# Side splits on GpSimd's queue, the second memory's K/V product at the first norm boundary, and index queries first in the mixing

## The chip, the cores and the metric

The kernel is one program on one core of a Trainium2 chip. The metric is device microseconds (us) of one execution. Matrix products run on TensorE (PE); VectorE (DVE), ScalarE (ACT) and GpSimd (POOL) do the rest, and SyncE (SP) issues most of the DMAs. Each engine takes its instructions in program order and waits at the head of its own queue; an instruction that cannot start holds up all behind it on that engine.

## The reference, cut to what matters

Two transformer blocks run one after the other on 512 tokens of width 1024, all in float32:

```python
h = rmsnorm(x, g_pre_mix)                    # block one
proj = h @ w_in                              # conv, q, k, v, memory q, three gates
merged = sigmoid(ga)*y_a + sigmoid(gb)*y_b + sigmoid(gc)*y_c
x = x + rmsnorm(merged @ w_out, g_post_mix)  # first norm boundary
h = rmsnorm(x, g_pre_ffn)
u = causal_dwconv(h @ w_up, ffn_conv_w, ffn_conv_b)
x = x + rmsnorm((gelu(a) * g) @ w_down, g_post_ffn)
h = rmsnorm(x, norm_mix)                     # block two
hq, hf, hi, hg, sq, sk, sv, iq, ik, iw, mq = split(h @ w_in_2)
o_hg = hgrn2_mix(hq, hf, hi, hg)             # gated recurrence
o_sa = dsa_mix(sq, sk, sv, iq, ik, iw)       # index scores choose the keys
o_mem = mem_mix(mq, rmsnorm(mem_2), w_mem_kv_2)
x = x + concat(o_hg, o_sa, o_mem) @ w_out_2
x = x + (silu(a) * b) @ w_ffn_out_2
```

## The kernel before, in words

Every float32 product is made of three TensorE passes over parts (L175 to L177): each operand is split into a rounded "hi" and the rest "lo". `load` (L189) brings a 512 KB weight tile into `r`, one of three raw buffers, on SP's queue. `split` then makes `wh` on ACT (L203) and `wl` on DVE (L204); there are three pairs of them. A raw buffer is free again when its `wl` is made, and a pair is free when TensorE is done with the tile three before.

The class `Program` holds the work as a list of jobs, which set the order in which instructions are written out. Before each job it splits weights up to two tiles ahead (four for the resident tiles of a `head_chunks`, six for those at the end of a `gemm_out`) and loads up to three more. A job writes its matrix product in pieces; after each piece comes a tick (`tick`), at which every background generator started by `pr.start(name, gen, rate)` takes `rate` steps. One tick is 6 matrix passes of 512 columns. `pr.drain(name)` steps the generators, with nothing between the steps, until that one has ended.

The weights of block two's mixing are split ahead of time, as side work: `Parts.make` (L212) loads a tile (L216), waits four steps, splits it on ACT (L218) and DVE (L219), waits three steps, writes both parts to a DRAM buffer `wd` (L221, L222) and the generator `splits` adds two steps. So a tile takes 9 ticks. When the mixing uses such a tile, `split` loads its parts from `wd` (L199, L200).

The stages around the change, with their place in the profiled execution: the third gate pass (378 to 441 us: eight times a gate chunk of 24 passes and a `w_mem_out` chunk of 12, with six side splits in the background, then `pr.drain("splits")`), `w_out` (441 to 494), the first norm boundary, the up projection (44 chunks of 24 passes, to 796, with 23 more side splits), the down projection, the second norm boundary, and the mixing (936 to 1195). A norm boundary: the last four jobs of `gemm_out` each end one 128-token tile, whose `epi1` normalises it (ACT L260, POOL L251, DVE L341). `next_head` then runs the first four chunks in two halves of 256 columns, and the transposes of the last two token tiles (L330) come inside it. The second memory's rows are normalised and transposed by `memT2.build`, started at up chunk 2; their K/V product `w_mkv2` (48 passes) runs at up chunk 6, after `pr.drain("memT2")`. In the up projection POOL makes the hi part of each result (L183), on which DVE's L180 waits.

Of the kernel before, what the change touches and what calls it, by code (L numbers as in the profile page):

```python
# [143 lines left out]
def body(tc, ctx, io):  # L144
# [62 lines left out]
    class Parts:  # L207
# [5 lines left out]
        def make(self):  # L213
            raw, hi, lo = slot([P, 1024]), slot([P, 1024], F32R), slot([P, 1024], F32R)
            self.d = drp.tile([2, P, 1024], F32, name=nm("wd"))
            nc.sync.dma_start(raw, self.src)  # L216
            yield from wait(4)
            a_.copy(hi, raw)  # L218
            v_.tensor_tensor(out=lo, in0=raw, in1=hi.bitcast(F32), op=ALU.subtract)  # L219
            yield from wait(3)  # L220
            nc.sync.dma_start(self.d[0], hi.bitcast(F32))  # L221
            nc.sync.dma_start(self.d[1], lo.bitcast(F32))  # L222

    pr = Program(load, split)

# [608 lines left out]
    def gate(br, m, use):  # L834
        def f(ps):
            th = tmp()
            a_.activation(th, ps, AF.Tanh, scale=0.5, bias=hbg[:, br * 8 + m:br * 8 + m + 1])
            st["th"] = th
        chunk(io["w_in_gate"][br * 8 + m], H, f)
        x = (cvx, oT, omT)[br]  # L840
        chunk(io[("w_conv_out", "w_attn_out", "w_mem_out")[br]][m], lambda: x, use, nk=4)
# [8 lines left out]
    def use_bc(m, last):  # L850
        def f(ps):
            z, dst = tmp(), mg[m // 2][:, m % 2, :]
            v_.scalar_tensor_tensor(z, st.pop("th"), 1.0, ps, op0=ALU.add, op1=ALU.mult)
            g_.tensor_tensor(out=dst, in0=dst, in1=z, op=ALU.add)
            if last:
                merged.put(m, dst)
        return f
# [23 lines left out]
    M = {n: [Parts(io[n][j]) for j in range(io[n].shape[0])]  # L881
         for n in ("w_hf", "w_hq", "w_iq", "w_mqsv", "w_sqk", "w_hi", "w_hg")}
    M["w_ikw"] = [Parts(io["w_ikw"])]
    order = [M[n][c] for n in ("w_hf", "w_hq") for c in (0, 1)] + M["w_ikw"] + M["w_iq"] + M["w_mqsv"]
    order += [M[n][c] for n in ("w_hf", "w_hq") for c in (2, 3)] + M["w_sqk"] + M["w_hi"] + M["w_hg"]

    def splits(a, b):
        def g():
            for p in order[a:b]:
                yield from p.make()  # L890
                yield from wait(2)
        return g
# [1 line left out]
    for m in range(KD):  # L894
        gate(1, m, use_bc(m, False))
    pr.drain("mem")
    pr.start("splits", splits(0, 6))
    for m in range(KD):
        gate(2, m, use_bc(m, True))
    pr.drain("splits")  # L900


    def post_norm(gpost, gpre, half):

        d = {}

        def setup():
            d["sq"] = cst.tile([P, NT], F32, name=nm("sqA"))
            d["hn"] = Act(KD)

        def epi0(t, ps):
            if t == 0:
                setup()
                d["post"], d["pre"] = load_gain(gpost), load_gain(gpre)
            if t % 2 == 0:
                d["f", t // 2] = slot([P, 2, 512])
            a_.activation(tmp(), ps, AF.Square, scale=half / 32, accum_out=d["sq"][:, t:t + 1])
            v_.tensor_tensor(out=d["f", t // 2][:, t % 2, :], in0=ps, in1=d["post"][:, 0:512], op=ALU.mult)

        def epi1(t, ps):  # L920
            sqB = small(1)
            a_.activation(tmp(), ps, AF.Square, scale=half / 32, accum_out=sqB)
            rs = rsqrt_small(1, [d["sq"][:, t:t + 1], sqB], 1.0, post=None if half == 1.0 else half)
            f1 = tmp()
            v_.tensor_tensor(out=f1, in0=ps, in1=d["post"][:, 512:D], op=ALU.mult)
            sq = []
            for hf, f in ((0, d["f", t // 2][:, t % 2, :]), (1, f1)):
                x = xs[t][:, hf * 512:hf * 512 + 512]
                v_.scalar_tensor_tensor(x, f, rs, x, op0=ALU.mult, op1=ALU.add)
                sq.append(ssq(x, 1 / 32))  # L930
            ys[t] = norm_y(xs[t], sq, d["pre"])

        def late(t):
            norm_T(ys.pop(t), put_h(d["hn"], t))

        def swap():
            st["h"] = d["hn"]
        return epi0, epi1, late, swap

    def next_head(late, srcs, uses, after=None):  # L940

        hooks = {(0, 0): late[1], (0, 2): lambda: late[0](2), (0, 3): lambda: late[0](3)}
        if after is not None:
            hooks[1, 1] = after
        head_chunks(srcs, H, uses, hooks)

    e0, e1, late, swap = post_norm("g_post_mix", "g_pre_ffn", 0.5)
    gemm_out(lambda hf, j: io["w_out"][hf * 4 + j], 4, lambda: merged, e0, e1, late=late)

# [11 lines left out]
    def use_up_a(j):  # L961
        def f(ps):
            ff[j] = ffn_conv(j, ps)
            a_.activation(ff[j], ff[j], AF.Gelu_apprx_tanh)
        return f
# [6 lines left out]
        return f  # L972

    W = io["w_up"]
    next_head((late, swap), [W[0], W[NFF], W[1], W[NFF + 1]], [use_up_a(0), use_up_g(0), use_up_a(1), use_up_g(1)])
    pr.start("splits", splits(6, len(order)))
    for j in range(2, NFF):
        if j == 2:
            pr.start("memT2", lambda: memT2.build())
        if j == 6:  # L980
            pr.drain("memT2")
            gemm_N([io["w_mkv2"][i] for i in range(4)], lambda: memT2, lambda t, ps: use_mkv2(t, ps), nt=2)
            pr.start("kv2", lambda: fin_mkv2())
        chunk(W[j], H, use_up_a(j))
        chunk(W[NFF + j], H, use_up_g(j))

# [512 lines left out]


    def mixing():
        next_head((late2, swap2), [M[n][c] for n in ("w_hf", "w_hq") for c in (0, 1)],
                  [use_hf(0), use_hf(1), use_hq(0), use_hq(1)], park)
        pr.start("gates0", gates(0))
        pr.start("hgrn", hgrn_levels, 0.6)
        chunk(M["w_ikw"][0], H, use_ikw)
        pr.start("idx", chain(sel0, index_weights, *(index_scores(c) for c in range(4)), top_keys(3),
                              top_keys(2), top_keys(1)), 1.0)
        for c in range(4):
            chunk(M["w_iq"][c], H, use_iq(c))  # L1510
        gemm_N(M["w_mqsv"], H, use_mqsv)
        pr.ctl(load_kv2)
        pr.start("finm", fin_mq)
        for c in (2, 3):
            chunk(M["w_hf"][c], H, use_hf(c))
        pr.drain("finm")
        pr.start("mem2", chain(mem2_pair(0), mem2_pair(1)), 0.5)
        for c in (2, 3):
            chunk(M["w_hq"][c], H, use_hq(c))
        pr.start("gates1", gates(1))  # L1520
        gemm_N(M["w_sqk"], H, use_sqk)
        pr.start("fin", fin_sqk)
        gemm_N(M["w_hi"], H, use_hi)
        pr.start("tail0", hgrn_tail(0))
        pr.start("sa", chain(sa_pair(0), sa_pair(1)), 0.5)
        pr.start("tail1", hgrn_tail(1))
        for c in range(4):
            chunk(M["w_hg"][c], H, use_hg(c))
# [180 lines left out]
```

## Time and profile before

| what | value |
|---|---|
| median of 3 runs | 1606.48 us (1604.28 to 1608.55) |
| the profiled execution | 1602.35 us |
| its span, first to last instruction | 1600.6 us |
| TensorE busy | 1533.0 us, 96% of the span |
| VectorE / ScalarE / GpSimd busy | 786.4 / 595.9 / 185.3 us |
| mean granted TensorE clock | 0.98 |
| DMA | 215.82 MB, mean 135 GB/s |

TensorE is busy nearly all the time, so a saving has to come from its idle time, from its time at the lower clock (a granted clock of 0.5 is 1.2 GHz, 1.0 is 2.4 GHz), or from fewer passes. What matters of the other engines is whom they keep waiting.

### The profile page before, as it was taken

The numbers are of one execution on the slowest core, as the hardware profiler recorded it, in microseconds if no ns is written. First come the engines' busy times: TensorE is split into PE (matmuls) and PEld (weight loads), VectorE is DVE, ScalarE is ACT, GpSimd is POOL, SyncE is SP. The second block draws the span as 40 slices with busy tenths as digits, with TensorE's granted clock in tenths as the row PEclk, the third lists the DMA queues.
The fourth block names the chain that finished last, engine by engine and source line by source line (L and its number), as shares of the span: only waits on it lengthen the run. The fifth ranks groups of instructions, "written<-read, shape, count | busy, mean of one in ns | idle before, by whom it ended". The sixth has DMA issues, their size and how long they took to land.

```text
span 1600.6 us, 20603 instructions
## 1 busy us (share of the span) xinstructions
PE 1533.0 (96%) x8107; PEld 1265.8 (79%) x8107; DVE 786.4 (49%) x1216; ACT 595.9 (37%) x1039; POOL 185.3 (12%) x325
## 2 busy tenths in 40 slices
PE   8999999999998889988999999998989999999999
PEld 7887888888778768767878897776868988888887
DVE  5455454554355666565633337996455333333231
ACT  5454453443344434333423245444543222222120
POOL 1000000131112100000000115434200000000000
PEclk9999999999999989999999999998999999999999
DMA  5322233323652356654565523432323222222331
GB/s 186 105 93 86 79 126 119 105 82 136 217 208 69 132 192 230 209 197 177 205 233 200 224 86 128 176 141 98 112 94 117 71 101 93 99 98 93 105 119 53
DMA packets 63623, 215.82 MB, mean 135 GB/s; under 512 B 7428, under 2 KB 7940, under 8 KB 63526
## 3 DMA queue, kind: packets, MB, share of 16 engines
q1 hardware_dynamic: 59040, 206.60, 36.4%
q10 hardware_dynamic: 4486, 7.90, 1.8%
q8 instruction: 64, 1.05, 0.3%
q14 instruction: 33, 0.27, 0.1%
HBM read 177.64 MB, written 36.83 MB: 134 GB/s over the span
## 4 chain that ended last, share of the span: by engine, by line
PE 39%; DVE 6%; DMA 4%; ACT 4%; issue 2%; POOL 2%; SPq 0%; ACTq 0%; POOLq 0%; DVEq 0%
PE p L175 12%; PE p L176 12%; PE p L177 12%; DMA s<-w_sqk 2%; DMA s<-w_hi 1%; DVE wl L204 1%; PE p L330 1%; DVE s L1053 1%; DMA s<-w_hq 1%; DVE m L1052 1%; ACT s L218 1%; ACT s L615 0%; POOL m L251 0%; DVE s L219 0%; POOL s L183 0%
## 5 line engine op out<-in xcount | busy, mean ns | idle before, releaser
L175 PE MATMUL p<-s,wh 128*128 128x512 f32 (+1 forms) x1224 | 481.0, 393 | 5.6 <-ACT wh L203 5.5
L177 PE MATMUL p<-s,wl 128*128 128x512 f32 (+1 forms) x1224 | 476.6, 389 | 8.8 <-DVE wl L204 8.8
L176 PE MATMUL p<-s,wh 128*128 128x512 f32 (+1 forms) x1224 | 475.9, 389 | 0.0
L204 DVE TENSOR_TENSOR wl<-r,wh 128x1024 fp32r<-128x1024 f32 x208 | 245.3, 1184 | 273.4 <-ACT wh L203 272.6
L177 PEld LDWEIGHTS p<-s,wl 128*128 128x128 f32 x1224 | 231.6, 189 | 59.2 <-DVE wl L204 11.7
L203 ACT CAST wh<-r 128x1024 fp32r<-128x1024 f32 x208 | 206.1, 996 | 191.6 <-PE p L176 180.2
L175 PEld LDWEIGHTS p<-s,wh 128*128 128x128 f32 x1224 | 231.8, 189 | 53.2 <-ACT wh L203 7.3
L176 PEld LDWEIGHTS p<-s,wh 128*128 128x128 f32 x1224 | 231.7, 189 | 44.7
L175 PE MATMUL p<-wh,s 128*128 128x512 f32 x512 | 207.3, 405 | 6.5 <-ACT wh L203 5.3
L176 PE MATMUL p<-wl,s 128*128 128x512 f32 x512 | 204.6, 400 | 7.7 <-DVE wl L204 7.7
L177 PE MATMUL p<-wh,s 128*128 128x512 f32 x512 | 203.8, 398 | 0.0
L176 PE MATMUL p<-s,s 128*128 128x256 f32 (+1 forms) x408 | 132.0, 324 | 4.6 <-DVE s L180 4.6
L175 PE MATMUL p<-s,s 128*128 128x256 f32 (+1 forms) x408 | 133.0, 326 | 2.2 <-ACT s L291 2.1
L177 PE MATMUL p<-s,s 128*128 128x256 f32 (+1 forms) x408 | 131.4, 322 | 0.0
L175 PEld LDWEIGHTS p<-wh,s 128*128 128x128 f32 x512 | 98.9, 193 | 29.6 <-ACT wh L203 6.2
L176 PEld LDWEIGHTS p<-wl,s 128*128 128x128 f32 x512 | 99.0, 193 | 29.2 <-DVE wl L204 9.3
L177 PEld LDWEIGHTS p<-wh,s 128*128 128x128 f32 x512 | 98.8, 193 | 21.2
L183 POOL TENSOR_SCALAR s<-t 128x512 fp32r<-128x512 f32 (+1 forms) x64 | 34.6, 541 | 663.2 <-DVE t L1574 227.4
L176 PEld LDWEIGHTS p<-s,s 128*128 128x128 f32 x408 | 79.4, 194 | 10.9 <-DVE s L180 5.6
L175 PEld LDWEIGHTS p<-s,s 128*128 128x128 f32 x408 | 79.2, 194 | 8.4 <-ACT s L291 2.8
L219 DVE TENSOR_TENSOR s<-s,s 128x1024 fp32r<-128x1024 f32 x29 | 35.5, 1225 | 101.4 <-ACT s L218 101.4
L177 PEld LDWEIGHTS p<-s,s 128*128 128x128 f32 x408 | 79.3, 194 | 5.4
(182 smaller groups left out, 1420.9 us busy)
## 6 DMA issues: line engine op xcount, KB each, us to landing
wd<-s SPq DMA_DIRECT2D x58, 512.0 KB, 5.3
r<-w_up SPq DMA_DIRECT2D x44, 512.0 KB, 4.1
r<-w_ffn_in SPq DMA_DIRECT2D x44, 512.0 KB, 3.2
wh<-wd SPq DMA_DIRECT2D x25, 512.0 KB, 3.5
wl<-wd SPq DMA_DIRECT2D x25, 512.0 KB, 4.4
r<-w_in_gate SPq DMA_DIRECT2D x24, 512.0 KB, 3.3
r<-w_down SPq DMA_DIRECT2D x22, 512.0 KB, 4.1
r<-w_ffn_out SPq DMA_DIRECT2D x22, 512.0 KB, 3.2
```

The lines of the kernel that those rows point to most:

```text
L175: mm(out, sh, mh, start=start, stop=False)
L176: mm(out, sh, ml, start=False, stop=False)
L177: mm(out, sl, mh, start=False, stop=stop)
L183: g_.tensor_scalar(out, x, s, 0.0, op0=ALU.mult, op1=ALU.add)
L203: a_.copy(hi[:, :n], raw)
L204: v_.tensor_tensor(out=lo[:, :n], in0=raw, in1=hi[:, :n].bitcast(F32), op=ALU.subtract)
L218: a_.copy(hi, raw)
L219: v_.tensor_tensor(out=lo, in0=raw, in1=hi.bitcast(F32), op=ALU.subtract)
L330: pe.transpose(ps[:m, n:n + P], s, ident)
L1052: v_.max(m8, sc)
L1053: v_.match_replace(sc, m8, sc, -BIG)
```

## The change

It does five things. The three DMAs of a side split go to GpSimd's queue instead of SP's. The order of the side splits starts with `w_ikw` and the four `w_iq` tiles, and eight of them, not six, are made in the third gate pass. `memT2` is built in that gate pass, from its fourth gate on. The `w_mkv2` product stands between `w_out` and the up projection, and the head of the up projection (`filled_head`) has two chunks instead of four, with the transposes of token tiles 2 and 3 ahead of its first and second piece. In the mixing, the head holds `w_ikw` and three `w_iq` tiles; the index generators start right after it, at rate 0.85 (it was 1.0), and the recurrence `hgrn` at 0.7 (it was 0.6); the `w_hf` and `w_hq` chunks follow.

```diff
@@ class Parts, make
-            nc.sync.dma_start(raw, self.src)
+            nc.gpsimd.dma_start(raw, self.src)
...
-            nc.sync.dma_start(self.d[0], hi.bitcast(F32))
-            nc.sync.dma_start(self.d[1], lo.bitcast(F32))
+            nc.gpsimd.dma_start(self.d[0], hi.bitcast(F32))
+            nc.gpsimd.dma_start(self.d[1], lo.bitcast(F32))
@@ order of the side splits
-    order = [M[n][c] for n in ("w_hf", "w_hq") for c in (0, 1)] + M["w_ikw"] + M["w_iq"] + M["w_mqsv"]
+    order = M["w_ikw"] + M["w_iq"] + [M[n][c] for n in ("w_hf", "w_hq") for c in (0, 1)] + M["w_mqsv"]
@@ third gate pass
-    pr.start("splits", splits(0, 6))
+    pr.start("splits", splits(0, 8))
     for m in range(KD):
+        if m == 3:
+            pr.start("memT2", lambda: memT2.build())
         gate(2, m, use_bc(m, True))
     pr.drain("splits")
+    pr.drain("memT2")
@@ first norm boundary
+    def filled_head(late, srcs, uses):
+
+        def first():
+            late[0](2)
+            late[1]()
+        head_chunks(srcs, H, uses, {(0, 0): first, (0, 1): lambda: late[0](3)})
+
@@ up projection
-    next_head((late, swap), [W[0], W[NFF], W[1], W[NFF + 1]], [use_up_a(0), use_up_g(0), use_up_a(1), use_up_g(1)])
-    pr.start("splits", splits(6, len(order)))
-    for j in range(2, NFF):
-        if j == 2:
-            pr.start("memT2", lambda: memT2.build())
-        if j == 6:
-            pr.drain("memT2")
-            gemm_N([io["w_mkv2"][i] for i in range(4)], lambda: memT2, lambda t, ps: use_mkv2(t, ps), nt=2)
-            pr.start("kv2", lambda: fin_mkv2())
+    gemm_N([io["w_mkv2"][i] for i in range(4)], lambda: memT2, lambda t, ps: use_mkv2(t, ps), nt=2)
+    filled_head((late, swap), [W[0], W[NFF]], [use_up_a(0), use_up_g(0)])
+    pr.start("kv2", lambda: fin_mkv2())
+    pr.start("splits", splits(8, len(order)))
+    for j in range(1, NFF):
@@ mixing
-        next_head((late2, swap2), [M[n][c] for n in ("w_hf", "w_hq") for c in (0, 1)],
-                  [use_hf(0), use_hf(1), use_hq(0), use_hq(1)], park)
+        next_head((late2, swap2), M["w_ikw"] + M["w_iq"][:3], [use_ikw, use_iq(0), use_iq(1), use_iq(2)], park)
+        pr.start("idx", chain(sel0, index_weights, *(index_scores(c) for c in range(4)), top_keys(3),
+                              top_keys(2), top_keys(1)), 0.85)
+        pr.start("hgrn", hgrn_levels, 0.7)
+        chunk(M["w_iq"][3], H, use_iq(3))
+        for c in (0, 1):
+            chunk(M["w_hf"][c], H, use_hf(c))
+        for c in (0, 1):
+            chunk(M["w_hq"][c], H, use_hq(c))
         pr.start("gates0", gates(0))
-        pr.start("hgrn", hgrn_levels, 0.6)
-        chunk(M["w_ikw"][0], H, use_ikw)
-        pr.start("idx", chain(sel0, index_weights, *(index_scores(c) for c in range(4)), top_keys(3),
-                              top_keys(2), top_keys(1)), 1.0)
-        for c in range(4):
-            chunk(M["w_iq"][c], H, use_iq(c))
```

Where this moves instructions, at three places.

ACT at the end of the third gate pass and the start of `w_out`. Before (L316 ends the gate pass, L218 is a side split; 3667, 3707, 3736 and 3770 are the four tiles that `w_out` streams first):

```order
L203 CAST wh_3667<-r_3579 128x1024 [waits DMAHW1_49,DVE_49,PE_49]
L837 ACTIVATE t_3700<-p_3673,hbg 128x512 [waits PE_49]
L203 CAST wh_3707<-r_3606 128x1024 [waits DMAHW4_49,DVE_49]
L316 CAST s_3729<-s_2141 128x512 [waits Pool_49]
L218 CAST s_3703<-s_3702 128x1024 [waits DMAHW2_49]
L203 CAST wh_3736<-r_3644 128x1024 [waits DMAHW6_49,DVE_49,PE_49]
L203 CAST wh_3770<-r_3671 128x1024 [waits DMAHW7_49,DVE_49,PE_49]
```

Now (the same four tiles are 3731, 3771, 3818 and 3852):

```order
L203 CAST wh_3731<-r_3643 128x1024 [waits DMAHW2_49,DVE_49,PE_49]
L837 ACTIVATE t_3764<-p_3737,hbg 128x512 [waits PE_49]
L203 CAST wh_3771<-r_3670 128x1024 [waits DMAHW3_49,DVE_49]
L316 CAST s_3793<-s_2141 128x512 [waits DMASW7_49,Pool_49]
L218 CAST s_3767<-s_3766 128x1024 [waits DMASW7_49,DMASW0_49]
L218 CAST s_3801<-s_3800 128x1024 [waits DMASW2_49]
L218 CAST s_3810<-s_3809 128x1024 [waits DMASW5_49]
L203 CAST wh_3818<-r_3708 128x1024 [waits DMAHW4_49,DVE_49,PE_49]
L203 CAST wh_3852<-r_3735 128x1024 [waits DMAHW5_49,DVE_49,PE_49]
```

Three side splits in a row, not one, stand between the second and the third tile of `w_out`.

DVE at the first norm boundary, from the last token tile's epilogue on. Before (the two `wl` are tiles of the up projection, used after the head):

```order
L925 TENSOR_TENSOR t_4146<-p_3912,s_3855 128x512
L929 SCALAR_TENSOR_TENSOR s_109<-s_3878,m_4144,s_109 128x512
L929 SCALAR_TENSOR_TENSOR s_109<-t_4146,m_4144,s_109 128x512
L341 SCALAR_TENSOR_TENSOR s_4160<-s_109,m_4157,s_3857 128x512 x2
L204 TENSOR_TENSOR wl_4164<-r_3901,wh_4163 128x1024
L204 TENSOR_TENSOR wl_4170<-r_3907,wh_4169 128x1024
```

Now (4234 and 4254 are the third and fourth tile of `w_mkv2`, 4260 and 4266 the two resident tiles of the head):

```order
L928 TENSOR_TENSOR t_4216<-p_3988,s_3937 128x512
L932 SCALAR_TENSOR_TENSOR s_109<-s_3960,m_4214,s_109 128x512
L932 SCALAR_TENSOR_TENSOR s_109<-t_4216,m_4214,s_109 128x512
L341 SCALAR_TENSOR_TENSOR s_4230<-s_109,m_4227,s_3939 128x512 x2
L204 TENSOR_TENSOR wl_4234<-r_3880,wh_4233 128x1024
L204 TENSOR_TENSOR wl_4254<-r_3977,wh_4253 128x1024
L204 TENSOR_TENSOR s_4260<-r_3983,s_4259 128x1024
L204 TENSOR_TENSOR s_4266<-r_4237,s_4265 128x1024
```

The first two tiles of `w_mkv2` are split before this epilogue, the other two behind it.

SP in the up projection, before (L216, L221 and L222 are a side split's DMAs):

```order
L189 DMA r_5419<-w_up 128x1024 [waits DMAHW6_49,DMAHW5_49,DVE_49]
L189 DMA r_5460<-w_up 128x1024 [waits DMAHW0_49,DVE_49]
L221 DMA wd_5396<-s_5394 128x1024 [waits DMAHW7_49]
L222 DMA wd_5396<-s_5395 128x1024
L216 DMA s_5483<-w_hq 128x1024 [waits DMAHW1_49]
L189 DMA r_5503<-w_up 128x1024 [waits DMAHW3_49,DMAHW2_49,DVE_49]
```

POOL there, now:

```order
L183 TENSOR_SCALAR s_5423<-t_5380 128x512 [waits DVE_49]
L221 DMA wd_5366<-s_5364 128x1024 [waits DMASW4_49,Activation_49]
L222 DMA wd_5366<-s_5365 128x1024 [waits DMASW5_49]
L216 DMA s_5453<-w_sqk 128x1024 [waits DMASW6_49]
L183 TENSOR_SCALAR s_5507<-t_5464 128x512 [waits DMAHW3_49,DVE_49]
```

The side split's DMAs no longer stand behind the weight loads that wait for DVE; they stand between POOL's L183.

## Rows read from the trace of the kernel before

**Rows 1.** The page: busy time, share and instructions of each engine.

```profile
PE 1533.0 (96%) x8107; PEld 1265.8 (79%) x8107; DVE 786.4 (49%) x1216; ACT 595.9 (37%) x1039; POOL 185.3 (12%) x325
```

**Rows 2.** Stretches: us, busy us (count) of PE, PEld, DVE, ACT, POOL; clock; DMA.

```profile
378.40:441.30 62.90, 61.36 (x269) 49.91 (x267) 25.98 (x31) 22.65 (x31) 7.73 (x6) 1.00 0.58 200
441.30:452.00 10.70, 6.81 (x18) 5.02 (x18) 4.87 (x6) 3.70 (x5) 2.53 (x2) 0.68 0.46 157
493.90:506.00 12.10, 7.78 (x51) 7.55 (x51) 8.43 (x15) 6.22 (x16) 3.28 (x7) 0.86 0.01 2
540.00:551.00 11.00, 5.05 (x24) 4.48 (x24) 4.95 (x8) 6.00 (x13) 2.17 (x4) 0.69 0.58 222
578.60:600.00 21.40, 15.97 (x48) 12.18 (x49) 13.54 (x15) 7.83 (x10) 1.81 (x4) 0.76 0.61 208
620.00:816.00 196.00, 179.54 (x749) 144.89 (x748) 115.23 (x134) 72.30 (x88) 9.29 (x15) 0.95 0.56 200
960.00:972.00 12.00, 9.02 (x36) 6.77 (x35) 6.73 (x10) 5.13 (x9) 6.57 (x15) 0.86 0.25 90
```

**Rows 3.** Waits of TensorE, 610 to 830 us: total us, times, longest.

```profile
PE p L177 <- DVE wl L204: 8.2, 5, 3.8
PE p L175 <- ACT wh L203: 4.5, 2, 3.8
PE p L176 <- DVE wl L204: 3.6, 1, 3.6
```

**Rows 4.** Waits of SP's queue, 600 to 830 us.

```profile
SPq L189 <- DVE wl L204: 164.6, 34, 11.2
```

**Rows 5.** The chain that ended last, around 690 us: start, us, what.

```profile
684.54 7.38 DMA s<-w_hq
691.94 1.06 ACT s L218
...
697.92 1.23 DVE wl L204
```

**Rows 6.** DMA issues: line, count, KB each, median us to landing.

```profile
r<-w_ffn_in SPq DMA_DIRECT2D x44, 512.0 KB, 3.2
...
s<-w_hf SPq DMA_DIRECT2D x4, 512.0 KB, 5.3
```

**Rows 7.** ACT in order of time, end of the third gate pass.

```profile
438.82 1.05 ACT L218 CAST s<-s 128x1024 fp32r<-128x1024 f32 x1 [6.85 <-DMA s<-w_ikw]
...
454.03 1.05 ACT L218 CAST s<-s 128x1024 fp32r<-128x1024 f32 x1 [3.86 <-DMA s<-w_iq]
454.99 2.00 ACT L203 CAST wh<-r 128x1024 fp32r<-128x1024 f32 x2
```

**Rows 8.** TensorE in order of time at the first norm boundary.

```profile
496.07 0.39 PE L175 MATMUL p<-s,s 128*128 128x256 f32 x1 [2.14 <-ACT s L291]
498.64 0.58 PE L176 MATMUL p<-s,s 128*128 128x256 f32 x1 [2.18 <-DVE s L180]
```

**Rows 9.** ACT and DVE in order of time, same place.

```profile
502.17 1.98 ACT L203 CAST wh<-r 128x1024 fp32r<-128x1024 f32 x2
...
503.33 1.41 DVE L341 SCALAR_TENSOR_TENSOR s<-s,m,s 128x512 f32<-128x512 f32 x2 [1.84 <-POOL m L251]
...
504.66 1.22 DVE L204 TENSOR_TENSOR wl<-r,wh 128x1024 fp32r<-128x1024 f32 x1
```

**Rows 10.** The DMAs on `wd`: issue time in ns, min/median/max.

```profile
L222 SPq DMA_DIRECT2D wd<-s x29: 326/424/1901, 389.7 to 857.3; - x29
```

**Rows 11.** POOL's instructions, 620 to 816 us, with its idle time.

```profile
L183 POOL TENSOR_SCALAR s<-t 128x512 fp32r<-128x512 f32 x15 | 9.3, 619 | 182.8 <-DVE t L970 122.8 <-issue 34.1 <-ACT t L956 13.9
```

**Rows 12.** Waits of DVE, 620 to 816 us.

```profile
DVE s L180 <- POOL s L183: 11.9, 15, 0.9
```

**Rows 13.** Waits of TensorE, 830 to 1195 us.

```profile
PE p L330 <- ACT s L624: 4.6, 1, 4.6
...
PE p L1461 <- POOL s L183: 1.5, 1, 1.5
```

## Prediction

> **What bounds the kernel now.** I read the page first: TensorE is busy 96% of the span [rows 1], so only its idle time, its time at 1.2 GHz and its number of passes can give anything. Then the table of stretches, around the places that the change touches: each such place has idle time, and then a stretch at a granted clock of 0.5 that the idle time brought on [rows 2]. I price a place as its length less its busy time, plus the lost share of the clock, less what of that share fell into the idle time. In the window at 494 us that is 12.1 − 7.78 = 4.3 us idle and 0.14 × 12.1 = 1.7 us of clock: 6.0. At 540 us (TensorE waits for the rows of `memT2`): 5.95 idle, 0.31 × 11 = 3.4 of clock, about half of it while idle: 7.7. At 579 (`w_mkv2`): 5.4 idle and 5.1 of clock: 10.5. From 620 to 816, the up projection and the start of the down projection beside the side splits: 16.3 of waits for `wh` and `wl` [rows 3] and 0.05 × 196 = 9.8 of clock, some 2 of it while idle: 24. At 441 (start of `w_out`): 3.9 and about 2.8: 6.7. At 960 (index scores): 3.0 and 1.4: 4.4 [rows 2]. Together about 59 us lie where the change works.
>
> Why TensorE waits for `wl` in the up projection is in SP's waits and in the chain. SP stands 164.6 of 230 us before a weight load L189, until DVE's `wl` frees a raw buffer [rows 4]. A side split's load stands behind it, lands 7.4 us after its late issue, holds ACT at L218, and ACT's and DVE's next weight halves come behind that; their `wl` is what the next L189 waits for [rows 5]. It is a ring through SP's queue.
>
> **The side splits on POOL's queue.** The edge from `wl` over SP to the side load is cut. On POOL the load stands behind the splits before it and behind L183, which runs once for each pair of chunks and needs 0.62 us [rows 11]. One tick is 6 passes: the third gate pass makes 288 passes in 61.4 us busy [rows 2], 0.213 each, so 1.28 us a tick, and a load has 4 ticks or 5.1 us until ACT asks for it. Against landing times of 3.2 to 7.4 us [rows 5, 6] that leaves ACT waits of up to 2.3 us, where `wh` is made two tiles or 10 us ahead. So I count nearly all of the 24 us as gained: −22, with ends of −24 and 0. What a DMA costs POOL no row shows. SP's issues take 0.42 us, at most 1.9 [rows 10]; I take about 1. Three of them and L183 are then 3.6 us in 9 ticks or 11.5 us, and L180, which waits 0.8 us for L183 today [rows 12], waits little longer.
>
> Here a rule speaks against the change. The Trainium skill (DMA: Bandwidth & Descriptors, Issuing engines are not separate DMA queues) says that DMAs from several engines share the same 16 DMA engines, and that issuing from another saves only the sequencer's time to start it. By that rule the move is worth 0.42 us for each of 87 DMAs of a queue that is on no path, and the term is 0. This trace disagrees in one point: it is not the starting that SP spends its time on but waiting, with the side load behind it.
>
> **The end of the third gate pass.** The 6.7 us at 441 and the 1.5 us that TensorE stands in the pass itself (62.90 − 61.36 [rows 2]) come from L218's wait for late loads (6.85 us for `w_ikw` [rows 7]); with loads on POOL I count −8 (ends 0 and −8). Against that stand two more side splits. Eight times 9 ticks are 72, the pass has 48, so three splits come in one row on ACT, between the second and third tile of `w_out`. They run in series: POOL issues a load only behind the stores of the split before, which wait for DVE. Let T be the end of the pass. The first L218 runs at about T + 3, when the last merged gate is out and its load has landed. Each further one is a copy (1.06), DVE's lo (1.23), two stores (0.8) and a load away: with 5.3 us to landing [rows 6] 8.4 us, so the third copy starts at T + 19.8 and the third tile's `wl` is made 3.5 us later, T + 23.3. TensorE has 48 passes ahead, 10.2 us. It stands about 13 us, and then runs for some time at 1.2 GHz: 3 us, as behind the 3.9 us at 441. Today's trace shows one link of this: the single L218 at 454.0 and the next `wh` at 455.0, 13.6 us behind the end of the pass [rows 7], which TensorE only just did not feel. +16, with ends of +9 (landing in 3.2 us, clock as here) and +21 (7.4 us).
>
> **`memT2` and `w_mkv2`.** Both leave the up projection: −7.7 − 10.5 = −18.2; the 48 passes themselves stay. In the gate pass the rows of `memT2` have the same 11 ticks (14.1 us) from load to transposes, and the loads stay on SP, behind one weight load. At 540 they came 6 us late with SP held for long; I take half with its clock, +3 (ends 0 and +7.7).
>
> **The first norm boundary.** The 48 passes, 10.2 us, are to cover the 6.0 us that are lost there. But only two of the four `w_mkv2` tiles are split ahead. Those last 5.1 us from the end of `w_out` at 493.9, to 499.0. ACT is through the last epilogue at 502.2, and DVE makes a `wl` only behind L341: from 504.66 on, 1.2 us each, to 507.0 for two [rows 9]. I expect TensorE to stand from 499 to 503, one pass, then until 505.9: 6.7 us, and 2 of clock. Then the second transposes' lo parts (L180) stand behind two more `wl`: 1.5. Together 10 against 6.0 today [rows 8]: +4, with ends of −6 (the tiles come in time) and +6.
>
> **The mixing.** The index scores no longer follow their queries at once: −4.4. The recurrence starts later and ends earlier in the order; the wait for POOL at L1461 (1.5 [rows 13]) should go. The last 4.6 us, for the softmax of the second pair on ACT, keep their place. The order is new throughout, so: −6, with ends of −12 and +6. The head with two chunks instead of four turns 96 half passes of 256 columns into 48 full ones; at 0.213 us a full one and, by choice, a tenth more than half of it for a half one, that is −1.
>
> **The sum.** −22 − 8 + 16 − 18.2 + 3 + 4 − 6 − 1 = −32. Against the profiled execution, 1602.35 us (span 1600.6 and 1.75 around it), that is 1570; that execution is 4.1 us under the median of 1606.48, and the forecast, for a median, is 1574.
>
> **The rivals.** *The covers hold.* Loads on a free queue land in 3.2 us, the row of splits costs 9 and not 16, the fill at the boundary works (−5 instead of +4), and the mixing gives 10: −52, or 1554. For it: a lone load lands so fast [rows 6]. Against: stores stand in front of each load.
>
> *The queue gives nothing.* The loads are late on POOL as on SP, since stores and L183 hold them and the same 16 DMA engines, busy 56% in that stretch [rows 2], carry them; ACT goes on waiting at L218. Without 18 of the 22 us: −14, or 1592. The rule above would have it so, and its time would be near this. Against: what made the side load late in the chain was its issue behind an L189 [rows 4, 5].
>
> *POOL becomes the bound: slower.* If a DMA costs POOL c us, a split takes 3c + 0.6 of its 11.5 us. From c = 3.6 on L183 is late, DVE's L180 behind it, and then `wl` and TensorE. 21 splits are stretched by 3c − 10.9 each, and the 22 us are not gained; the gain is used up at (32 + 22) : 21 = 2.6 us a split, c = 4.5. At c = 5 it is 86 + 22 − 32, or about 1680; at 4.6, 1610. Against: that is ten times what SP's issue takes [rows 10]. For: POOL's issue is nowhere in this trace. The Trainium skill (SBUF — State Buffer, Who interferes with whom) says that DVE can lock GpSimd out of writing descriptors in its two-port modes, and that `tensor_tensor`, which has none, contends with its reads alone; DVE's L204, 1.2 us for 1024 columns, is one, and the trace cannot show more.
>
> **How the numbers follow.** Forecast 0.50 (1562 to 1586 by the smaller terms), covers hold 0.20, the queue gives nothing 0.20, POOL the bound 0.10. A measurement tells 0.3%, 5 us, from no change. The range takes the forecast, most of the first two rivals and none of the last: 1553 to 1599. Faster by over 0.3% are the first three cases but for 0.03: 0.87; within, 0.04; slower, 0.09.
>
> **What would show it.** Right: SP's L189 without side DMAs behind it, waits for `wh` and `wl` between 620 and 816 us under 3 us, a wait of 10 to 16 us on ACT's `wh` in `w_out`, one of 4 us or more in `w_mkv2`, none at the first index scores. Wrong: `w_out` without a gap, ACT still waiting at L218 in the up projection, or POOL without idle time there.

## The result and the profile after

The changed kernel takes 1581.8 us, a median of 4 runs (1576.8 to 1585.9), against 1607.1 us (1604.3 to 1608.6) for the kernel before in the same comparison: a ratio of 0.9843, 95% interval 0.9812 to 0.9875. That is 25 us less where 32 were forecast, and 1574 with its range of 1553 to 1599 holds it.

The profiled execution of the changed kernel took 1585.87 us (span 1584.1). It is the slowest of its four runs, 4 us above the median, and that of before is 5 us below its own, so the two traces differ by 16.5 us where the medians differ by 25. 3.4 us of this spread lie in the first 136 us, which the change doesn't touch (the same TensorE wait begins at 132.47 us in one trace and at 135.82 in the other). Places are compared below by the traces, sizes by the runs.

The first line of the page of the changed kernel, to be read beside [rows 1]: POOL alone has more work, 45 us and 87 instructions, which are the DMAs it now issues.

```profile
PE 1522.5 (96%) x8059; PEld 1259.2 (79%) x8059; DVE 786.8 (50%) x1216; ACT 596.2 (38%) x1039; POOL 230.5 (15%) x412
```

The table of stretches of the changed kernel, with the columns of [rows 2]: the third gate pass, the start of `w_out` behind it, the first boundary with `w_mkv2` in it, 196 us of the up projection and the down projection's start beside the side splits, and two places in the mixing.

```profile
394.30:457.30 63.00, 61.87 (x278) 50.13 (x276) 31.61 (x39) 26.89 (x42) 19.96 (x26) 1.00 0.70 242
457.30:476.00 18.70, 6.83 (x16) 5.03 (x16) 6.01 (x6) 5.97 (x6) 2.65 (x5) 0.63 0.63 222
507.20:526.10 18.90, 14.44 (x51) 11.08 (x50) 11.12 (x16) 7.88 (x19) 3.94 (x9) 0.82 0.35 108
600.00:796.00 196.00, 196.00 (x866) 162.32 (x865) 133.93 (x154) 86.13 (x103) 36.05 (x65) 1.00 0.66 229
976.00:988.00 12.00, 6.65 (x19) 4.99 (x18) 10.63 (x26) 5.38 (x14) 10.61 (x26) 0.72 0.52 209
1130.00:1145.00 15.00, 8.76 (x74) 7.76 (x73) 3.21 (x8) 5.88 (x11) 1.18 (x4) 0.77 0.10 35
```

The fourth row is the gain: 196.00 us busy of 196, at full clock, where before there were 179.54 of 196 and 0.95. The second row is a price: 11.9 us idle at the start of `w_out`, then half clock. The last two are another: waits in the mixing that the kernel before has not at this size. TensorE's waits in the changed kernel, first 380 to 600 us (all of them), then 915 to 1180 us (the longest):

```profile
PE p L175 <- ACT wh L203: 13.5, 2, 11.2
PE p L176 <- DVE wl L204: 2.8, 2, 2.2
PE p L177 <- DVE wl L204: 1.6, 1, 1.6
PE p L330 <- DVE s L341: 1.1, 2, 0.6
PE p L330 <- DVE s L1095: 1.1, 1, 1.1
```

```profile
PE p L1467 <- POOL s L183: 6.2, 1, 6.2
PE p L1343 <- ACT s L1326: 5.4, 1, 5.4
PE p L1368 <- DVE s L1334: 4.8, 1, 4.8
PE p L330 <- ACT s L624: 4.0, 1, 4.0
```

Adding up, for each stretch, TensorE's idle time and half of the time at 1.2 GHz in which it was not idle gives the balance below (us; worked out from the gaps between its instructions and the granted clock). The third column is the kernel before with the new queue alone, the first experiment.

| stretch | before | queue alone | changed kernel |
|---|---|---|---|
| third gate pass and `w_out` | 8.2 | 0.1 | 16.4 |
| first boundary | 6.0 | 3.9 | 7.5, with `w_mkv2` |
| rows of `memT2` | 7.9 | 7.5 | in the gate pass |
| `w_mkv2` | 10.3 | 5.1 | in the boundary |
| up projection, start of the down projection | 24.9 | 0.0 | 2.7 |
| second boundary | 0.8 | 0.8 | 0.8 |
| mixing | 25.7 | 23.7 | 41.0 |
| sum | 83.8 | 41.1 | 68.4 |

So by the traces the queue alone takes away 43 us of loss, and the rest of the change gives 27 back (21 to 23 by the runs below). The part at 1.2 GHz differs from one execution to the next. Four traces have the mixing's code of the changed kernel: its own and those of splits7, splits5 and queue_back below. Their idle time in it is 27.5, 25.8, 27.7 and 27.8 us, their loss by the half clock 13.5, 15.4, 7.9 and 11.0. So the 41.0 of the mixing is good to some 5 us.

### The profile page after: what moved, and what is told of

Read it like the earlier page. It is cut to its first block, busy times and chain, and to the rows that moved or that the text cites. A ratio compares the mean times of both kernels' runs of the same rounds, so it can differ in the third digit from the quotient of the medians.

```text
span 1584.1 us, 20561 instructions
## 1 busy us (share of the span) xinstructions
PE 1522.5 (96%) x8059; PEld 1259.2 (79%) x8059; DVE 786.8 (50%) x1216; ACT 596.2 (38%) x1039; POOL 230.5 (15%) x412
## 4 chain that ended last, share of the span: by engine, by line
PE 78%; DVE 6%; ACT 5%; POOL 4%; issue 4%; DMA 3%; ACTq 0%; DVEq 0%; SPq 0%; POOLq 0%
PE p L175 24%; PE p L176 24%; PE p L177 24%; PE p L330 2%; DMA s<-w_mqsv 1%; PE p L641 1%; DMA s<-w_iq 1%; POOL m L251 1%; ACT t L260 1%; POOL s L183 1%; PE p L1467 1%; PE p L581 1%; POOL m L248 1%; PE p L582 1%; ACT s L615 1%
## 5 line engine op out<-in xcount | busy, mean ns | idle before, releaser
L175 PE MATMUL p<-s,wh 128*128 128x512 f32 (+1 forms) x1240 | 485.4, 391 | 0.0
L204 DVE TENSOR_TENSOR wl<-r,wh 128x1024 fp32r<-128x1024 f32 x210 | 248.0, 1184 | 299.5 <-ACT wh L203 298.7
L203 ACT CAST wh<-r 128x1024 fp32r<-128x1024 f32 x210 | 208.5, 997 | 210.2 <-PE p L176 197.4
L175 PEld LDWEIGHTS p<-s,wh 128*128 128x128 f32 x1240 | 233.7, 188 | 46.5 <-issue 0.7
L175 PE MATMUL p<-wh,s 128*128 128x512 f32 x512 | 205.1, 401 | 14.9 <-ACT wh L203 13.5
L175 PEld LDWEIGHTS p<-wh,s 128*128 128x128 f32 x512 | 98.2, 192 | 37.2 <-ACT wh L203 14.3
L176 PE MATMUL p<-s,s 128*128 128x256 f32 (+1 forms) x376 | 122.3, 325 | 2.4 <-DVE s L180 2.4
L175 PE MATMUL p<-s,s 128*128 128x256 f32 (+1 forms) x376 | 123.5, 328 | 0.0
L177 PE MATMUL p<-s,s 128*128 128x256 f32 (+1 forms) x376 | 121.9, 324 | 0.0
L183 POOL TENSOR_SCALAR s<-t 128x512 fp32r<-128x512 f32 (+1 forms) x64 | 34.5, 539 | 583.5 <-DVE t L1581 227.4
L176 PEld LDWEIGHTS p<-s,s 128*128 128x128 f32 x376 | 72.6, 193 | 8.6 <-DVE s L180 3.3
L175 PEld LDWEIGHTS p<-s,s 128*128 128x128 f32 x376 | 72.7, 193 | 5.9 <-ACT s L291 0.3
L177 PEld LDWEIGHTS p<-s,s 128*128 128x128 f32 x376 | 72.6, 193 | 5.3
L180 DVE TENSOR_TENSOR s<-p,s 128x256 fp32r<-128x256 f32 (+1 forms) x102 | 46.9, 506 | 58.5 <-ACT s L316 32.5
```

What stands on the lines that cost most here:

```text
L175: mm(out, sh, mh, start=start, stop=False)
L176: mm(out, sh, ml, start=False, stop=False)
L177: mm(out, sl, mh, start=False, stop=stop)
L180: v_.tensor_tensor(out=out, in0=x, in1=hi.bitcast(F32), op=ALU.subtract)
L183: g_.tensor_scalar(out, x, s, 0.0, op0=ALU.mult, op1=ALU.add)
L203: a_.copy(hi[:, :n], raw)
```

## The experiments

Medians of 4 runs each. The kernel before had medians of 1605 to 1609 us in these comparisons, so differences between kernels of different comparisons are good to some 4 us. "Fill" stands for the rows of `memT2` in the gate pass and `w_mkv2` in the first boundary.

| kernel | queue | splits in the pass | fill | mixing | us | ratio to before, 95% |
|---|---|---|---|---|---|---|
| changed kernel | GpSimd | 8 | both | new | 1581.8 | 0.9843 (0.9812 to 0.9875) |
| queue_only | GpSimd | 6 | none | old | 1560.4 | 0.9716 (0.9690 to 0.9742) |
| queue_back | SyncE | 8 | both | new | 1627.7 | 1.0135 (1.0109 to 1.0161) |
| loads_only | GpSimd, loads | 6 | none | old | 1556.9 | 0.9701 (0.9681 to 0.9722) |
| act_queue | ACT | 6 | none | old | 1556.1 | 0.9697 (0.9682 to 0.9712) |
| memt_early | GpSimd | 6 | `memT2` | old | 1556.4 | 0.9675 (0.9658 to 0.9693) |
| splits7 | GpSimd | 7 | both | new | 1572.9 | 0.9794 (0.9777 to 0.9810) |
| splits5 | GpSimd | 5 | both | new | 1563.0 | 0.9743 (0.9708 to 0.9778) |
| mix_old | GpSimd | 8 | both | old | 1570.8 | 0.9776 (0.9748 to 0.9804) |
| hgrn_late | GpSimd | 8 | both | new, levels later | 1581.8 | 0.9827 (0.9805 to 0.9848) |
| hgrn06 | GpSimd | 8 | both | new, rate 0.6 | 1573.0 | 0.9796 (0.9781 to 0.9810) |
| s5_mixold | GpSimd | 5 | both | old | 1550.9 | 0.9637 (0.9618 to 0.9657) |
| s5_idx | GpSimd | 5 | both | old, scores later | 1549.4 | 0.9632 (0.9615 to 0.9649) |

### The queue alone, put in and taken out

queue_only is the kernel before with three lines changed; queue_back is the changed kernel with the same three changed back.

```diff
-            nc.sync.dma_start(raw, self.src)
+            nc.gpsimd.dma_start(raw, self.src)
...
-            nc.sync.dma_start(self.d[0], hi.bitcast(F32))
-            nc.sync.dma_start(self.d[1], lo.bitcast(F32))
+            nc.gpsimd.dma_start(self.d[0], hi.bitcast(F32))
+            nc.gpsimd.dma_start(self.d[1], lo.bitcast(F32))
```

> The kernel before with one edit: the three DMAs of each side split are issued by GpSimd instead of SyncE. Theory (a ring through SP's queue made the weight halves late): the 17.0 us of TensorE idle time and 7.9 us of half clock between 607 and 830 us go, and with SP free of side loads some of the 13.4 us at 540 and 579 us may go too: ratio to before 0.976 to 0.986, about 1570 to 1585 us. Rival (the same DMA engines carry the same bytes, so the queue gives nothing, and the stalls went because the second memory's work left the up projection): within 0.3% of before.

> The changed kernel with one edit: the side splits' DMAs are back on SyncE's queue. Theory (ring through SP): the waits for wl and wh return to the up projection, 17 us idle and 8 us of half clock, so about 25 us over the changed kernel: 1600 to 1610 us, ratio to before about 1.00. Rival (queue gives nothing): no change against the changed kernel, 1578 to 1587 us, ratio 0.982 to 0.988.

Measured: 45 us less when it is put in, and 46 us more when it is taken out of the changed kernel. The move is worth the same in both settings, and the rest of the change, at eight splits and with the new mixing, costs 21 to 23 us in both. The expectations had 20 to 35 us for putting it in and 25 for taking it out: the mechanism held, the size was larger. The trace of queue_back says where: it loses 33 us more than that of the changed kernel in the up projection and the start of the down projection, and 9 more in the third gate pass and `w_out`, of which the expectation had nothing.

SP's waits between 600 and 830 us in queue_only:

```profile
SPq L189 <- DVE wl L204: 206.6, 43, 9.2
SPq L189 <- DMA r<-w_down: 3.2, 1, 3.2
```

SP's and then TensorE's waits in queue_back, 600 to 840 us:

```profile
SPq L189 <- DVE wl L204: 175.8, 37, 11.6
SPq L221 <- ACT s L218: 11.7, 4, 3.7
```

```profile
PE p L177 <- DVE wl L204: 10.8, 9, 3.7
PE p L175 <- ACT wh L203: 6.9, 5, 2.5
PE p L176 <- DVE wl L204: 3.9, 1, 3.9
```

With the new queue SP waits even longer before L189 than in [rows 4], and TensorE has no wait at all in that window (queue_only and the changed kernel alike). In these traces a weight load that waits for its buffer costs TensorE nothing when no side load stands behind it. With the queue put back the waits of [rows 3] return, 21.6 us of them.

### Which of the three DMAs, and which queue

loads_only moves only the first of the three lines to GpSimd and leaves both stores on SyncE. act_queue writes `nc.scalar` in place of `nc.sync` in all three.

> The kernel before with only the load of each side split on GpSimd's queue; its two stores stay on SyncE. Theory (it is the load that stands behind L189 on SyncE, as the prediction had it): nearly the whole 45 us of queue_only, ratio 0.970 to 0.978. Rival (the stores on SyncE, which wait for ACT's copy and DVE's difference, hold the next weight loads behind them, and the load is only late in consequence): the gain is mostly absent, ratio 0.990 to 1.000, and TensorE still waits for wl in the up projection.

> The kernel before with all three DMAs of a side split on ACT's queue in place of SyncE's. Theory (what counts is that SyncE's queue is left, not that it is GpSimd): a gain as with GpSimd less what ACT loses, since the store of the difference makes ACT wait about 1.2 us for DVE's L219 in each of 29 splits, beside TensorE's work: ratio 0.970 to 0.980. Rival (ACT is the weight halves' engine, and standing for stores holds up wh): ratio above 0.985, with TensorE waiting for wh.

Both give the whole gain (48 and 49 us; not told apart from queue_only). SP's waits in loads_only, 600 to 830 us:

```profile
SPq L189 <- DVE wl L204: 187.2, 43, 7.0
SPq L222 <- DVE s L219: 2.2, 4, 0.9
SPq L221 <- ACT s L218: 1.8, 2, 1.1
```

The stores wait 4.0 us in all, and TensorE waits for nothing in this window. It is the load behind L189 that made the ring, as the prediction had it: to move it is enough. (The counterpart, the stores moved and the load left on SyncE, was not run.) That ACT's queue does as well as GpSimd's rules out that GpSimd is the point, and ACT's waits for DVE's difference there (L203 and L956 behind L219) come to 5.4 us, which TensorE doesn't feel:

```profile
ACT t L956 <- DVE s L219: 3.7, 2, 2.9
ACT wh L203 <- DVE s L219: 1.7, 2, 1.2
```

### Splits beside the third gate pass

```diff
-    pr.start("splits", splits(0, 8))
+    pr.start("splits", splits(0, 5))
...
-    pr.start("splits", splits(8, len(order)))
+    pr.start("splits", splits(5, len(order)))
```

splits7 has 7 in both places.

> The changed kernel with five side splits instead of eight beside the third gate pass (45 of its 48 ticks), the other 24 beside the up projection. Theory (three splits in a row on ACT at the pass's end hold the third tile of w_out): the 11.2 us wait at 457 us and the half clock behind it, 15 us together, go: about 1567 us, ratio to before 0.975. Rival (the third tile is late for another reason, such as its own load, or the three splits cost as much beside the up projection): 1576 to 1586 us, ratio 0.981 to 0.987, with the wait still there or waits for wh and wl in the up projection.

> The changed kernel with seven side splits beside the third gate pass instead of eight. Theory (each split that doesn't fit in the 48 ticks costs one row of copy, difference, stores and load, about 8 us, of which the first two thirds are covered by the 10.2 us of passes ahead): the wait of 11.2 us at 457 us shrinks to 3 to 5 us: 1568 to 1574 us, ratio 0.977. Rival (the drain costs the same once more than one split is left over): 1580 us.

Fewer splits beside the pass take less time: 1581.8 (eight), 1572.9 (seven), 1563.0 (five); six were not run in the changed kernel. The links can be read from ACT and POOL at the end of the pass in the changed kernel (start, us, line, and in brackets the idle time before and its releaser). ACT first:

```profile
450.44 1.05 ACT L218 CAST s<-s 128x1024 fp32r<-128x1024 f32 x1 [0.31 <-DMA s<-w_hf]
458.49 1.04 ACT L218 CAST s<-s 128x1024 fp32r<-128x1024 f32 x1 [7.00 <-DMA s<-w_hf]
466.51 1.04 ACT L218 CAST s<-s 128x1024 fp32r<-128x1024 f32 x1 [6.98 <-DMA s<-w_hq]
467.46 1.99 ACT L203 CAST wh<-r 128x1024 fp32r<-128x1024 f32 x2
```

```profile
451.79 0.57 POOL L221 DMA_DIRECT2D wd<-s  x1 [2.31 <-ACT s L218]
453.05 0.53 POOL L222 DMA_DIRECT2D wd<-s  x1 [0.69 <-DMA r<-w_out]
453.57 0.54 POOL L216 DMA_DIRECT2D s<-w_hf  x1
```

Copy, difference, two stores, load, and 4.9 us until it has landed: the copies stand 8.05 and 8.02 us apart, and the `wh` of the third tile follows the last of them. TensorE's passes end at 457.34, and it stands until 468.55. TensorE's waits from 380 to 600 us in splits7, then in splits5:

```profile
PE p L175 <- ACT wh L203: 5.3, 2, 3.0
PE p L177 <- DVE wl L204: 3.2, 2, 1.6
PE p L176 <- DVE wl L204: 2.8, 2, 1.9
```

```profile
PE p L177 <- DVE wl L204: 2.5, 2, 1.7
PE p L176 <- DVE wl L204: 2.2, 1, 2.2
```

With seven the wait at `w_out` is down to 2.4 and 0.95 us, about as the 8 us of a row and 10.2 us of cover give it; with five it is gone. The second wait for `wh`, in the first boundary (2.3 us with eight, 3.0 with seven), is 0.5 us with five, so that fewer splits help there too; by which link, no view here shows. By the balance of the table above, splits5 loses 15 us less than the changed kernel in the gate pass and `w_out` and 3 less in the first boundary, close to the 19 us of the medians, and TensorE has no wait in its up projection, where the three splits went.

### The mixing

mix_old takes back the last hunk of the change, so that `mixing()` is that of before. hgrn_late and hgrn06 keep the new order and change one line each:

```diff
-        pr.start("hgrn", hgrn_levels, 0.7)
...
         pr.start("gates0", gates(0))
+        pr.start("hgrn", hgrn_levels, 0.7)
```

```diff
-        pr.start("hgrn", hgrn_levels, 0.7)
+        pr.start("hgrn", hgrn_levels, 0.6)
```

> The changed kernel with the mixing's order of the kernel before (recurrence queries first, index queries later, rates 0.6 and 1.0). Theory (the new order costs: 27.5 us idle and 13.5 us of half clock between 919 and 1178 us in the changed kernel against 18.1 and 7.5 before): 15 us less than the changed kernel, about 1567 us, ratio to before 0.975. Rival (the losses in the mixing are set by the work ahead of it, by DMA or by spread between executions): 1578 to 1586 us, ratio 0.983 to 0.987.

> The changed kernel with the recurrence's levels started behind gates0, as before, and all else of the new mixing kept. Theory (in the new order the levels' set-up is already done when the gates are, so that the first products stand 13 us behind the scans on DVE instead of 27, and TensorE waits for them): the wait of 5.4 us at 977 us and 3.4 us of half clock behind it go, 1573 us, ratio 0.979, and later waits stay. Rival (the recurrence only ends later, and what is won at its start is lost at its end, where TensorE waits 6.3 us for L183): 1580 us or more, with a longer wait at the output products.

> The changed kernel with the recurrence at its old rate, 0.6 instead of 0.7. Theory (the new order leaves the recurrence less room: 59 groups of six passes from its first products to the last output products instead of 80; at a lower rate it only ends later): no gain, 1580 to 1595 us, with a longer wait for L183 at L1467. Rival (the higher rate crowds DVE, ACT and GpSimd, so the 4.8 and 5.4 us waits inside the recurrence come from the rate): 1570 to 1575 us.

mix_old is 11 us faster than the changed kernel: the mixing's new form costs, it does not gain. hgrn_late changes nothing (1581.8), and the wait at the first products stays, at 6.1 us: my theory that the levels' set-up stands too early is wrong. hgrn06 is 9 us faster, and there my theory fell a second time: the new order has room for the old rate, and it was the rate of 0.7 that cost. (By the ratios the two steps are 11 and 8 us.) TensorE's longest waits in hgrn06, 910 to 1170 us:

```profile
PE p L1343 <- DVE s L1334: 4.3, 1, 4.3
PE p L581 <- DVE s L1474: 4.0, 1, 4.0
PE p L1368 <- DVE s L1334: 3.4, 2, 2.8
PE p L330 <- ACT s L624: 3.0, 1, 3.0
```

The wait for L183 at L1467 (6.2 us in the changed kernel) is not there any more, and that inside the recurrence (L1368) is smaller. How the first came about is in the changed kernel's DVE and POOL, 1128 to 1141 us:

```profile
1134.79 1.22 DVE L204 TENSOR_TENSOR wl<-r,wh 128x1024 fp32r<-128x1024 f32 x1 [4.73 <-ACT wh L203]
1135.93 0.29 DVE L1374 COPY_PREDICATED t<-lmask,p 128x128 f32<-128x128 uint32 x1
...
1138.16 0.29 DVE L1374 COPY_PREDICATED t<-lmask,p 128x128 f32<-128x128 uint32 x1
```

```profile
1138.55 1.36 POOL L183 TENSOR_SCALAR s<-t 32x128 f32<-32x128 f32 x4 [18.07 <-DVE t L1374]
```

The last mask copies of the recurrence stand on DVE behind a `wl`, whose `wh` stands on ACT behind the eight softmax instructions of L624 (1130.1 to 1133.7 us). At 0.6 the recurrence's end falls elsewhere in the order, and DVE's last L1374 is through at 1134.4 without this wait (hgrn06's DVE):

```profile
1131.94 1.23 DVE L204 TENSOR_TENSOR wl<-r,wh 128x1024 fp32r<-128x1024 f32 x1 [0.25 <-ACT wh L203]
1134.14 0.30 DVE L1374 COPY_PREDICATED t<-lmask,p 128x128 f32<-128x128 uint32 x1 [0.76 <-PE p L1368]
```

In idle time the mixing lost 22.0 us in hgrn06 against 25.8 to 27.8 in the four traces at 0.7, and in half clock 6.4 against 7.9 to 15.4. The step in idle time is clear of the spread of the four; how much of the clock is the rate's, one trace cannot tell. hgrn06 and mix_old, 1573.0 and 1570.8, are not told apart by their intervals: the new order of the queries, with the index generators at 0.85, in itself neither gains nor loses by what these runs can tell.

### The places of the second memory's work, and the repairs together

memt_early is queue_only with the rows of `memT2` beside the third gate pass, as in the changed kernel:

```diff
     for m in range(KD):
+        if m == 3:
+            pr.start("memT2", lambda: memT2.build())
         gate(2, m, use_bc(m, True))
     pr.drain("splits")
+    pr.drain("memT2")
...
-        if j == 2:
-            pr.start("memT2", lambda: memT2.build())
         if j == 6:
-            pr.drain("memT2")
```

s5_mixold is the changed kernel with five splits and the old mixing, and s5_idx is s5_mixold with the index scores started one chunk later:

```diff
         chunk(M["w_ikw"][0], H, use_ikw)
-        pr.start("idx", ...)
+        chunk(M["w_iq"][0], H, use_iq(0))
+        pr.start("idx", ...)
```

> The kernel before with the new queue and the rows of memT2 beside the third gate pass; w_mkv2 stays in the up projection, six splits, old mixing. Theory (with the side splits off SP the rows land in time in the gate pass): the wait of 4.9 us at 530 us with 2 us of half clock goes, and about 1 us of waits comes into the gate pass: 6 us under queue_only, 1554 to 1555 us, ratio 0.968. Rival (the rows are late wherever they are asked for, by 5 us): 1560 us, with the wait in the gate pass.

> The changed kernel with both repairs: five side splits beside the third gate pass and the mixing in the old order. Theory (the two losses lie apart, and add): 1581.8 less 18.8 (splits5) less 11.1 (mix_old), 1552 us, ratio to before 0.967, 8 us under the kernel before with the new queue alone, which is then what the places of the second memory's product and rows are worth. Rival (they overlap, so that one repair takes up what the other leaves): 1558 to 1563 us, no better than queue_only.

> The kernel s5_mixold with the index scores started one chunk later (behind the first w_iq chunk, in the old mixing order). Theory (TensorE waits 3.0 us for DVE's L569 only because the scores stand right behind their queries): that wait and 1.5 us of half clock go, 4 to 5 us under s5_mixold, about 1548 us. Rival (the top keys then come later and TensorE stands at the later places in their stead): same as s5_mixold within 2 us, or slower.

memt_early's median is 4 us under that of queue_only; by the ratios to the kernel before it is 6.6 us, and the two intervals touch, so that it is not clearly told apart from queue_only. The wait for L341 that it was to remove does shrink, from 4.8 to 0.6 us. TensorE's row for it in queue_only, then in memt_early, 380 to 600 us:

```profile
PE p L330 <- DVE s L341: 4.8, 1, 4.8
```

```profile
PE p L330 <- DVE s L341: 0.6, 1, 0.6
```

With its half clock the place of the rows lost 7.5 us in queue_only and loses nothing now; but the spans of the two traces differ by only 0.3 us, since that of memt_early loses 3 us more at the first boundary and 2 more each at `w_mkv2` and in the mixing. So the worth of the rows' place lies between nothing and 7 us.

s5_mixold comes to 1550.9: both repairs add (19 and 11 us alone, 31 together). It is 5.5 us under memt_early, with intervals that do not meet; that is the worth of `w_mkv2` in the boundary, of five splits instead of six, of their new order and of the head with two chunks together. It beats both kernels, the kernel before by 3.6%. s5_idx is level with it, as its rival had it: the wait of 3.0 us at the index scores is gone, and others, of 0.7 to 1.2 us at later places (L581 behind L1107, L175 behind L1095, L330 behind L679), stand in its place.

## Why the prediction was right, and where it was wrong

**The queue (−22).** Right in mechanism: the ring through SP, with the side load behind L189 as its link, is confirmed by the edit in both directions and by loads_only. In the stretch for which the term was made the trace gives −24.9. The forecast's other term for the queue, −8 for the gate pass, held as well: 8.2 became 0.1 in queue_only. But the edit alone gives −45, not −30. The forecast put 18.2 us down to the old places of `memT2` and `w_mkv2`; with the queue moved and nothing else, 5.2 of `w_mkv2`'s 10.3 went (3 to 6 in the four kernels that have it there with the queue moved). So the ring made weights late there too, where side splits also ran. Since `w_mkv2` leaves its place in the changed kernel in any case, the sum did not feel that this was booked under the wrong edit. Another 4.5 us went at the first boundary, at the rows and in the mixing; the 2.1 at the boundary are not there in loads_only (6.8 us lost, against 6.0 before), so these small ones are not shown to be the queue's.

**The rule against it.** The Trainium skill (DMA: Bandwidth & Descriptors, Issuing engines are not separate DMA queues) would have given 0. The runs differ from that by 45 us; the traces agree that the sequencer's own time is small (0.53 to 0.57 us for a DMA on POOL). What the rule leaves out here is the waiting of an issuing engine: 164.6 us before L189 [rows 4], with the DMAs behind it.

**The end of the gate pass (−8, +16).** Right, and by its own steps: 8.0 us from copy to copy where 8.4 were worked out, TensorE standing 11.9 us where it was about 13, and 3.4 of half clock where it was 3. By the runs the splits above five cost 19 us, with 3 of them at the first boundary by the traces.

**`memT2` and `w_mkv2` (−18.2 + 3).** In the trace −17.1: 1.1 us of waits in the gate pass instead of 3. As the worth of the edits it was too much: with the queue moved the rows' new place brings 7 us at most, and what came with `w_mkv2`'s 5.5.

**The first boundary (+4).** 7.5 against 6.0, so +1.5: the two unsplit tiles stand behind the last epilogue as read from [rows 9] (L341 at 515.10, `wl` at 516.43), but TensorE stands 4.5 us, not 6.7, and the L180 waits didn't follow.

**The mixing (−6, ends −12 and +6).** This step failed, in sign and beyond its ends: +15 by the trace, +11 by the runs. The wait at the index scores went, as predicted, and the wait for POOL, which "should go", grew from 1.5 to 6.2 us. The mistake was to price the places named in the waits of before, and to give "the order is new throughout" ±6 without looking at the rate: 0.6 became 0.7, and hgrn06 shows 9 of the 11 us there (8 of 11 by the ratios).

**The sum.** −32 was forecast and −25 measured, although the mixing alone was off by 17 (−6 forecast, +11 by the runs). The terms without it were forecast at −26 and came to −31 by the traces and −36 by the runs. So the total came out near in part by luck: the misses had opposite signs.

**The rivals.** POOL as the bound is out: 36.05 us busy of 196 in the up projection, and c is 0.53 to 0.57 us. The sums of that rival do not agree with each other: its 1680 at c = 5 counts the 22 us as lost out of the gain of 32; done the same way, only 10 us are left to be used up, at 0.5 us a split (c = 3.8, not 4.5), and c = 4.6 gives about 1657, not 1610. With c as measured this changes nothing. The queue giving nothing is out by queue_only and queue_back. The covers did not hold in the changed kernel (the row of splits, the mixing), but a kernel in which they mostly do takes 1551 to 1549 us, near the 1554 of that rival.

**The signs named ahead.** Waits for `wh` and `wl` in the up projection: none. A wait of 10 to 16 us for `wh` in `w_out`: 11.2. One of 4 us in `w_mkv2`: 2.3 and 2.2, in two. None at the first index scores: right. One sign was badly chosen: ACT still waits at L218, 32.4 us between 600 and 830 us in the changed kernel and 41.6 in queue_only, against 71.9 before, and up to 10.8 at once. TensorE feels none of it.

**What stays open.** Which part of the rate's 9 us is crowding on POOL, ACT and DVE, which the coming together with the softmax, and which the clock. Whether six splits would do as well as five, and what `w_mkv2` in the boundary is worth by itself. The head of the up projection with two chunks (−1) is too small to be seen.

## What to carry to other kernels

In a queue that is served in order, look for the wait that other DMAs stand behind, not for the queue's busy time: here one load for each side split, moved off the queue of the weight loads, was worth 45 to 49 us, and which of two other queues took it made no difference that the runs can tell. When one cause starves several places, price it by an edit that removes it alone, before its losses are booked under the edits that happen to move those places. In a hand-written order, a change of rate is an edit of its own: count for each engine what a faster rate puts side by side, above all where the chain's end meets another chain.

## What the runs showed of the hardware

A DMA of 512 KB issued by GpSimd holds POOL for 0.53 to 0.57 us (L216, L221 and L222 between 600 and 796 us in the changed kernel, below with POOL's L183 beside them), half of what was estimated:

```profile
L183 POOL TENSOR_SCALAR s<-t 128x512 fp32r<-128x512 f32 x17 | 10.4, 611 | 119.5 <-DVE t L980 119.5
L221 POOL DMA_DIRECT2D wd<-s x16 | 9.0, 562 | 19.6 <-ACT s L218 19.5 <-issue 0.2
L222 POOL DMA_DIRECT2D wd<-s x16 | 8.6, 539 | 18.3 <-DVE s L219 18.2
```

L183 stays at 0.61 us (0.62 before [rows 11]), and DVE's L204 has a mean of 1.221 us in this stretch and 1.222 in the kernel before: GpSimd's DMAs and DVE's `tensor_tensor` beside them did not slow each other measurably. 67 of the 87 DMAs in the changed kernel had a `tensor_tensor` of DVE beside them for over half of their time on POOL and took 0.55 us in the mean, as did the 8 with no DVE instruction beside them.

The time at the lower clock that came with a wait was not constant. In the changed kernel the granted clock was 0.5 for 13.7 us around the 11.2 us wait at `w_out`, and for 6.8 us at each of the waits of 5.4, 4.8, 6.2 and 4.0 us in the mixing. The same wait of 4.0 us (L330 for L624) had 3.4 us at 0.5 with it in splits5 and hgrn_late. So the half clock of one execution is no fixed price of a wait: with equal idle time in the mixing, 27.5 and 27.7 us, the changed kernel lost 13.5 us by it and splits5 7.9.
